# Dense products of a two-layer hybrid trunk: both correction passes in f16, with scaled weights and operands

## The chip, the cores and the metric

The kernel runs on one core of one Trainium2 chip. The metric is the device time of one execution in microseconds (us); less is better.

## What is computed

The reference takes x (1 x 512 x 1024, float32) through two layers. Cut to what matters:

```python
h = layer_norm(x, ln_in_g, ln_in_b)
for layer in range(2):
    proj = h @ w_in[layer]
    # split into the inputs of three mixers: retention, HGRN2, sliding-window attention
    y_a = (silu(rg) * r_o) @ ret_w_out[layer]
    y_b = (silu(hg) * h_o) @ hgrn_w_out[layer]
    y_c = s_o @ swa_w_out[layer]
    merged = sigmoid(ga) * y_a + sigmoid(gb) * y_b + sigmoid(gc) * y_c
    h = layer_norm(DN_ALPHA * h + merged @ w_o[layer], ln_mix_g[layer], ln_mix_b[layer])
    if layer == 0:
        ff = (silu(h @ w_gate) * (h @ w_up)) @ w_down          # dense, width 2816
    else:
        ff = top-2-of-8 experts of the same form               # width 3584
    h = layer_norm(DN_ALPHA * h + ff, ln_ffn_g[layer], ln_ffn_b[layer])
```

All weights arrive as float32 from DRAM.

## The kernel before, in words

Tokens are 512 = 4 blocks (j) of 128, D_MODEL is 8 slices (k) of 128. The residual stream is held transposed, as operand hT. To reach float32-like results, every dense operand is held in two parts: a high part, the value rounded to float32r (the type FR, which TensorE takes in one pass), and a low part, the remainder. A product is three matmuls into the same PSUM tile: high x high, high weight x low operand, low weight x high operand. mm3 (L347 to L350) issues these three; proj_t (L448) issues the same three itself at L457 to L459. I call three such matmuls a group. Before the change all three are float32r.

There are two forms of a product. proj_f (L418) holds a weight tile of 128 columns still and moves 512 tokens: 8 groups per tile. proj_t (L448) holds 128 tokens still and moves 512 weight columns: 32 groups (4 blocks x 8 slices) per product of depth 1024. proj_f_halves (L429) is used once, at the head of the FFN, with 256 tokens at a time; proj_t with 256 columns makes the values of the attention.

Weights come through the class Stream: SP loads a raw tile (L204, three buffers), and _prep (L211) makes its two parts: ScalarE writes whi with a Copy to float32r (L225), VectorE writes wlo as raw minus whi (L226). Five buffers of each part exist, and three tiles are prepared ahead. In the expert stage (the flag half) tiles are 2048 wide, scaled by WS, and wlo is f16 already (L221, L222); there the high parts run float32r and the low part of the weights runs f16, in blocks: accumulate (L1400) and by_row (L1459) issue all float32r matmuls of a tile first and then all f16 ones. by_row, used for the down projection of the last two experts, has eight float32r and four f16 matmuls of 512 columns per block.

Operands are split by split_evac (L343): ScalarE copies PSUM to the high part (L344), VectorE writes the low part (L345). It serves the transposed LayerNorm output (turn in ln_tile, L384), the branches of the three mixers (to_branch, L607, and the attention's values, L850). The merge (gate_merge, L900 and L901) and the FFN (L989 and L990) do the same from SBUF.

The order of TensorE's work is the order in which the code issues it: TensorE is in a manual schedule (L277). A helper (soon, tick) puts small attention and HGRN matmuls between products after a given amount of TensorE time. The order on ScalarE, VectorE and GpSimd is set by the scheduler of the tile framework. Each engine works its queue in order.

The program's stages: LayerNorm and the first product (to about 50 us), the attention of layer 0 (to about 200), HGRN heads (to about 400), gates, retention and merge (to 860), the dense FFN (to 1240), the same mixers for layer 1 (to 2080), and routing and experts (to the end). LayerNorm (ln_tile, L363) works on VectorE, ScalarE (L373) and GpSimd (L375, which adds ln_b); its blocks are transposed on TensorE (L388) when a product first needs them.

Of the kernel before, what the change touches and what calls it, by code (L numbers as in the profile page):

```python
# [21 lines left out]
P = 128  # L22
D = 1024
S = 512
# [33 lines left out]
XS = 1.0 / 64.0  # L58

# [127 lines left out]
class Stream:  # L187


    def __init__(self, nc, raw, parts, ahead, half):  # L190
        self.nc, self.raw, self.parts, self.ahead, self.half = nc, raw, parts, ahead, half
        self.todo, self.loaded, self.ready, self.held = [], [], [], 0

# [17 lines left out]
    def _prep(self):  # L211
# [7 lines left out]
        lo = pool.tile([P, width], F16 if self.half else FR, name="wlo", bufs=bufs)  # L219
        if self.half:  # L220
            nc.scalar.activation(hi[:, :n], raw, AF.Copy, scale=WS)  # L221
            nc.vector.scalar_tensor_tensor(lo[:, :n], raw, WS, hi[:, :n].bitcast(F32),  # L222
                                           op0=OP.mult, op1=OP.subtract)
# [26 lines left out]
def body(tc, A, out, dbg=None):  # L250
# [86 lines left out]
    V.memset(eps_ln, LN_EPS)  # L337
    eps_rms = const.tile([P, 1], F32, name="eps_rms")
    V.memset(eps_rms, RMS_EPS)
# [23 lines left out]
    def ln_tile(pool, j, r, gb, bb, hT, to_out, after=None, spread=False):  # L363
        mv = pool.tile([P, 4], F32, name="ln_mv", bufs=2)
        V.bn_aggr(mv[:, 0:2], stats[j])
        SC.activation(mv[:, 2:3], mv[:, 1:2], AF.Sqrt, bias=eps_ln)
# [17 lines left out]
        def turn():  # L384
            for kk in range(2):
                tp = psM.tile([P, 4, P], F32, name="mx")
                for k in range(4):
                    T.transpose(tp[:, k], r[:, (4 * kk + k) * P:(4 * kk + k + 1) * P], ident)  # L388
                split_evac(tp, hT[0][:, 4 * kk:4 * kk + 4, j * P:(j + 1) * P],
                           hT[1][:, 4 * kk:4 * kk + 4, j * P:(j + 1) * P])  # L390
# [17 lines left out]
    def new_hT():  # L408
        hi = hpool.tile([P, KD, S], FR, name="hThi")
        lo = hpool.tile([P, KD, S], FR, name="hTlo")  # L410
        return hi, lo
# [6 lines left out]
    def proj_f(hT, kn=KD):  # L418
        need(*range(NJ))
        whi, wlo = stream.next()  # L420
        ps = psA.tile([P, S], F32, name="acc")
        for k in range(kn):
            sl = slice(k * P, (k + 1) * P)
            mm3(ps, whi[:, sl], wlo[:, sl], hT[0][:, k], hT[1][:, k], k == 0, k == kn - 1)
# [4 lines left out]
    def proj_f_halves(hT, n):  # L429
# [6 lines left out]
        for th in range(2):  # L436
            tk = slice(256 * th, 256 * th + 256)
            for i, (ps, (whi, wlo)) in enumerate(zip(pss, ws)):
                if th == 0 and i >= n - 2:
                    need(i - n + 4)  # L440
                for k in range(KD):
                    sl = slice(k * P, (k + 1) * P)
                    mm3(ps[:, tk], whi[:, sl], wlo[:, sl], hT[0][:, k, tk], hT[1][:, k, tk], k == 0, k == KD - 1)
# [4 lines left out]
    def proj_t(xT, kn, per, n, done=None):  # L448
# [5 lines left out]
        def tile_(j, k, w, q):  # L454
# [3 lines left out]
            T.matmul(pss[j], xT[0][:, k, tj], w[1][:, sl], start=False, stop=False)  # L458
            T.matmul(pss[j], xT[1][:, k, tj], w[0][:, sl], start=False, stop=(k == kn - 1))  # L459
# [25 lines left out]
    def out_ln(pool, xT, kn, per, g_ap, b_ap, nxt, after=None):  # L485
# [3 lines left out]
        SC.dma_start(bb, rows(b_ap))  # L489
        old = hbuf[0]  # L490
# [8 lines left out]
        def done(j, ps):  # L499
            sl = slice(512 * half, 512 * half + 512)  # L500
            V.scalar_tensor_tensor(rs[j][:, sl], rs[j][:, sl], ALPHA, ps, op0=OP.mult, op1=OP.add)
# [24 lines left out]
    for j in range(NJ):  # L526
# [3 lines left out]
        if j == 0:  # L530
# [3 lines left out]
            SY.dma_start(bb, rows(A["ln_in_b"]))  # L534
        else:
# [38 lines left out]
    def route_consts():  # L574
# [6 lines left out]
        SC.activation(rt[:, :, 0], raw, AF.Copy)  # L581
        V.tensor_tensor(rt[:, :, 1], raw, rt[:, :, 0].bitcast(F32), OP.subtract)
# [10 lines left out]
        routing[:] = [rt, tri, tok, ones, iota, eidx]  # L593


    def gated_norm(pool, o_j, n, gate_j, width):
# [5 lines left out]
        SC.activation(ss[:, 1, :n], ss[:, 0, :n], AF.Sqrt, bias=eps_rms, scale=1.0 / width)  # L602
# [4 lines left out]
    def to_branch(gate, c0, br, k):  # L607
# [4 lines left out]
        split_evac(tf, br[0][:, k], br[1][:, k])  # L612
# [179 lines left out]
    def swa(pool, layer, hT, br):  # L792
# [14 lines left out]
        for j, ps in enumerate(proj_t(hT, KD, 4, 256)):  # L807
            SC.activation(v[:, j], ps, AF.Copy)
# [41 lines left out]
        def values(g, j, pts):  # L850
# [5 lines left out]
            split_evac(po[rp], br[0][rp, gp * GQ:(gp + 1) * GQ, j * P:(j + 1) * P],  # L856
# [812 lines left out]
```

## Time and profile before

| | us |
|---|---|
| median of 3 runs | 3213.3 |
| lowest and highest run | 3211.13, 3214.2 |
| the profiled execution, as timed | 3213.63 |
| its span, from first to last instruction | 3211.6 |
| TensorE busy in it | 3083.2 |
| VectorE busy | 2002.6 |
| ScalarE busy | 1665.6 |
| GpSimd busy | 744.9 |

The span is what the views of the trace divide up; 2.0 us of the profiled execution lie outside it. PE is TensorE's matmul side, PEld its weight loads, DVE is VectorE, ACT is ScalarE, POOL is GpSimd, SP issues the weight DMAs. Matmuls are pipelined: the time from one start to the next is shorter than the time one lasts, and it is the former that adds up.

### The profile page before, as it was taken

To read this page: it belongs to the slowest core of one execution; us is meant where nothing else is said; L and a number is where in the kernel's file an instruction comes from. 1 tells how busy PE (TensorE), PEld (TensorE's weight loads), DVE (VectorE), ACT (ScalarE), POOL (GpSimd) and SP (SyncE) were. 2 spreads that over 40 slices of the span, in tenths; PEclk is the share of its full clock that TensorE was granted. 3 is DMA by queue.
4 is the path that set the end of the run, shared out by engine and by line. 5 is a ranking of instruction groups with operands and counts; after the bars stand their busy time and mean duration, and the time that the engine had idled before them with its cause. 6 is when DMAs were issued, how large, how long until landed. Compare 5 with 4: busy or idle time off the path is not lost. (4 is left out here: it accounts for less than half of the span.)

```text
span 3211.6 us, 50454 instructions
## 1 busy us (share of the span) xinstructions
PE 3083.2 (96%) x20186; PEld 2666.9 (83%) x20186; DVE 2002.6 (62%) x2387; ACT 1665.6 (52%) x2475; POOL 744.9 (23%) x541
## 2 busy tenths in 40 slices
PE   7999899999999999999899999969999999999996
PEld 6778788888888888777788888869999999999794
DVE  5766733334533325766833334469888898989998
ACT  4655333323332214664433333248778787888785
POOL 1243501101100001234500111114223242242442
PEclk9999999999999999999999999979999999999998
DMA  5112132222422333111222222359999999999995
GB/s 175 53 56 83 56 105 89 82 92 92 147 99 99 117 115 110 63 59 53 79 92 92 88 83 93 117 196 350 332 326 347 331 343 350 361 341 379 384 374 203
DMA packets 108463, 562.60 MB, mean 175 GB/s; under 512 B 13115, under 2 KB 13163, under 8 KB 75965
## 3 DMA queue, kind: packets, MB, share of 16 engines
q1 hardware_dynamic: 96768, 522.23, 45.2%
q10 hardware_dynamic: 6732, 24.34, 2.0%
q0 software_dynamic: 4720, 12.72, 1.2%
q8 instruction: 161, 2.64, 0.3%
q14 instruction: 82, 0.66, 0.1%
HBM read 545.39 MB, written 13.85 MB: 174 GB/s over the span
## 5 line engine op out<-in xcount | busy, mean ns | idle before, releaser
L222 DVE SCALAR_TENSOR_TENSOR wlo<-raw,whi 128x2048 f16<-128x2048 f32 (+1 forms) x348 | 786.2, 2265 | 86.7 <-ACT whi L221 85.2
L225 ACT ACTIVATE whi<-raw 128x1024 fp32r<-128x1024 f32 x314 | 332.6, 1060 | 833.4 <-PE acc L294 712.4
L226 DVE TENSOR_TENSOR wlo<-raw,whi 128x1024 fp32r<-128x1024 f32 x314 | 435.6, 1388 | 510.3 <-ACT whi L225 486.3
L221 ACT ACTIVATE whi<-raw 128x2048 fp32r<-128x2048 f32 (+1 forms) x348 | 642.1, 1848 | 57.3 <-PE gu L294 50.7
L294 PE MATMUL acc<-hThi,whi 128*128 128x512 f32 (+1 forms) x1312 | 510.2, 389 | 2.3 <-ACT hThi L344 2.3
L294 PE MATMUL acc<-hTlo,whi 128*128 128x512 f32 (+1 forms) x1312 | 506.5, 386 | 1.4 <-DVE hTlo L345 1.4
L294 PE MATMUL acc<-hThi,wlo 128*128 128x512 f32 (+1 forms) x1312 | 506.2, 386 | 0.0
L294 PE MATMUL gu<-xg,whi 128*128 128x288 f32 (+6 forms) x3584 | 496.0, 291 | 6.0 <-DVE gt L1428 2.7
L294 PEld LDWEIGHTS gu<-xg,whi 128*128 128x128 f32 x3584 | 453.8, 190 | 7.9 <-ACT whi L221 3.2
L1432 POOL TENSOR_TENSOR gs<-gs,gt 128x288 f32<-128x288 f32 (+6 forms) x112 | 255.6, 2282 | 583.9 <-ACT gs L1431 583.6
L294 PEld LDWEIGHTS <-wlo 128*128 128x128 f16 x4928 | 285.2, 98 | 23.3 <-DVE wlo L222 6.0
L294 PEld LDWEIGHTS acc<-hThi,whi 128*128 128x128 f32 x1312 | 248.8, 190 | 55.2 <-issue 4.9
L294 PEld LDWEIGHTS acc<-hTlo,whi 128*128 128x128 f32 x1312 | 248.7, 190 | 49.3 <-DVE hTlo L345 1.7
L294 PEld LDWEIGHTS acc<-hThi,wlo 128*128 128x128 f32 x1312 | 248.4, 189 | 49.6
L294 PE MATMUL gu<-xh,wlo 128*128 128x144 f16 (+6 forms) x3584 | 244.6, 221 | 1.8 <-DVE wlo L222 1.4
L294 PE MATMUL acc<-whi,hThi 128*128 128x512 f32 (+1 forms) x576 | 224.9, 390 | 0.4 <-ACT hThi L344 0.3
L294 PE MATMUL acc<-whi,hTlo 128*128 128x512 f32 (+1 forms) x576 | 220.3, 383 | 3.9 <-DVE hTlo L345 3.9
L294 PE MATMUL acc<-wlo,hThi 128*128 128x512 f32 (+1 forms) x576 | 219.9, 382 | 2.0 <-DVE wlo L226 2.0
L294 PE MATMUL gu<-hd,whi 128*128 128x288 f32 (+4 forms) x1344 | 194.2, 295 | 0.0
L294 PEld LDWEIGHTS gu<-hd,whi 128*128 128x128 f32 x1344 | 174.9, 189 | 0.3
L294 PE MATMUL acc<-brhi,whi 128*128 128x512 f32 x384 | 150.0, 391 | 0.0
L294 PE MATMUL acc<-brhi,wlo 128*128 128x512 f32 x384 | 149.5, 389 | 0.0
(288 smaller groups left out, 4395.2 us busy)
## 6 DMA issues: line engine op xcount, KB each, us to landing
raw<-in_w_gu SPq DMA_DIRECT2D x224, 1024.0 KB, 7.2
raw<-in_w_l SPq DMA_DIRECT2D x248, 512.0 KB, 3.4
raw<-in_w_dn SPq DMA_DIRECT2D x96, 896.0 KB, 5.6
raw<-in_w_ffn SPq DMA_DIRECT2D x66, 512.0 KB, 3.5
raw<-in_w_dr SPq DMA_DIRECT2D x28, 1024.0 KB, 7.7
hspillm<-ln_r ACTq DMA_DIRECT2D x8, 512.0 KB, 2.6
ybuf<-ys ACTq DMA_DIRECT2D x5, 512.0 KB, 9.3
ln_r<-in_x SPq DMA_DIRECT2D x4, 512.0 KB, 10.9
```

The source lines that it names most:

```text
L221: nc.scalar.activation(hi[:, :n], raw, AF.Copy, scale=WS)
L222: nc.vector.scalar_tensor_tensor(lo[:, :n], raw, WS, hi[:, :n].bitcast(F32), op0=OP.mult, op1=OP.subtract)
L225: nc.scalar.activation(hi[:, :n], raw, AF.Copy)
L226: nc.vector.tensor_tensor(lo[:, :n], raw, hi[:, :n].bitcast(F32), OP.subtract)
L294: nc.tensor.matmul(out_, lhsT, rhs, start=start, stop=stop)
L1432: G.tensor_tensor(s, s, t[:, 1], OP.mult)
```

## The change

Dense weights are scaled by DS = 256 and operands by factors of LS = 16, so that remainders and copies fit f16. A weight tile now has three parts: whi (float32r), the remainder in f16 (the first half of the tile named wlo), and an f16 copy of the weight divided by LS (the second half of wlo). An operand has three parts as well: high (float32r), low (f16), and an f16 copy (named hT16, br16, hid16, fin16). mm3 and proj_t issue high x high in float32r, weight remainder x operand copy in f16, weight copy x operand remainder in f16. The producers of operands put the scales into constants that their instructions take: scales of LayerNorm and of the RMS norms, the factors of gates and FFN. The number of matmuls and their shapes stay the same. The expert stage changes in constants only.

```diff
@@ Stream._prep
         hi = pool.tile([P, width], FR, name="whi", bufs=bufs)
-        lo = pool.tile([P, width], F16 if self.half else FR, name="wlo", bufs=bufs)
+        lo = pool.tile([P, 2048], F16, name="wlo", bufs=bufs)
+        scale = WS if self.half else DS
+        nc.scalar.activation(hi[:, :n], raw, AF.Copy, scale=scale)
+        nc.vector.scalar_tensor_tensor(lo[:, :n], raw, scale, hi[:, :n].bitcast(F32), op0=OP.mult, op1=OP.subtract)
         if self.half:
...
+            self.ready.append((hi, lo))
         else:
-            nc.scalar.activation(hi[:, :n], raw, AF.Copy)
-            nc.vector.tensor_tensor(lo[:, :n], raw, hi[:, :n].bitcast(F32), OP.subtract)
-        self.ready.append((hi, lo))
+            if self.early:
+                nc.gpsimd.tensor_scalar(lo[:, 1024:1024 + n], raw, 1.0 / LS, None, op0=OP.mult)
+            else:
+                nc.scalar.activation(lo[:, 1024:1024 + n], raw, AF.Copy, scale=1.0 / LS)
+            self.ready.append((hi, lo, lo[:, 1024:]))
@@ body
-    def split_evac(ps, hi, lo, src_f32=None):
-        SC.activation(hi, ps, AF.Copy)
-        V.tensor_tensor(lo, ps, hi.bitcast(F32), OP.subtract)
-
-    def mm3(ps, whi, wlo, xhi, xlo, first, last):
-        T.matmul(ps, whi, xhi, start=first, stop=False)
-        T.matmul(ps, whi, xlo, start=False, stop=False)
-        T.matmul(ps, wlo, xhi, start=False, stop=last)
+    def split(src, hi, lo, x16):
+
+        SC.activation(hi, src, AF.Copy, scale=1.0 / (DS * LS))
+        SC.activation(x16, src, AF.Copy, scale=1.0 / (DS * LS))
+        V.scalar_tensor_tensor(lo, hi.bitcast(F32), -DS * LS, src, op0=OP.mult, op1=OP.add)
+
+    def mm3(ps, w, x, first, last):
+        T.matmul(ps, w[0], x[0], start=first, stop=False)
+        T.matmul(ps, w[1], x[2], start=False, stop=False)
+        T.matmul(ps, w[2], x[1], start=False, stop=last)
@@ proj_t
-            T.matmul(pss[j], xT[0][:, k, tj], w[1][:, sl], start=False, stop=False)
-            T.matmul(pss[j], xT[1][:, k, tj], w[0][:, sl], start=False, stop=(k == kn - 1))
+            T.matmul(pss[j], xT[2][:, k, tj], w[1][:, sl], start=False, stop=False)
+            T.matmul(pss[j], xT[1][:, k, tj], w[2][:, sl], start=False, stop=(k == kn - 1))
@@ out_ln, and the same line in the first norm
+        V.tensor_scalar(bb, bb, LS, None, op0=OP.mult)
@@ dense_ffn
-                V.tensor_tensor(t, pu, t, OP.mult)
-                SC.activation(hi[:, f], t, AF.Copy)
-                V.tensor_tensor(lo[:, f], t, hi[:, f].bitcast(F32), OP.subtract)
+                V.scalar_tensor_tensor(t, pu, LS, t, op0=OP.mult, op1=OP.mult)
+                split(t, hi[:, f], lo[:, f], x16[:, f])
```

The flag early is False and nothing sets it, so ScalarE makes the copy of every weight. In gate_merge and dense_ffn a tensor_tensor becomes a scalar_tensor_tensor with LS as its factor; the router gets an f16 copy of its weights.

The order of matmuls on TensorE is the same in both kernels, and so are SP's DMAs. What an f16 matmul adds is an instruction of its own that loads the held operand; there are 5184 of them. On TensorE, at the end of the first product (rows one to three of the first listing are the last group of proj_t, the rest the first of proj_f; mm3 has the same form), before:

```order
L294 MATMUL acc<-whi,hThi 128x512
L294 MATMUL acc<-wlo,hThi 128x512
L294 MATMUL acc<-whi,hTlo 128x512
L294 MATMUL acc<-hThi,whi 128x512
L294 MATMUL acc<-hTlo,whi 128x512
L294 MATMUL acc<-hThi,wlo 128x512
```

and in the changed kernel, where hT_89 is the f16 copy of hT:

```order
L302 MATMUL acc<-whi,hThi 128x512
L302 LDWEIGHTS hT_89
L302 MATMUL acc<-wlo,hT_89 128x512
L302 LDWEIGHTS hTlo
L302 MATMUL acc<-wlo,hTlo 128x512
L302 MATMUL acc<-hThi,whi 128x512
L302 LDWEIGHTS wlo
L302 MATMUL acc<-hT_89,wlo 128x512
L302 LDWEIGHTS wlo
L302 MATMUL acc<-hTlo,wlo 128x512
```

Every group is now one float32r matmul and two f16 ones, so the type changes twice in a group.

On VectorE, in the first LayerNorm (ln_r are the token blocks, ln_mv their statistics, hTlo the low parts of the transposed output), before:

```order
L365 BN_AGGR ln_mv<-ln_st 128x2
L345 TENSOR_TENSOR hTlo<-mx,hThi 128x4x128
L226 TENSOR_TENSOR wlo<-raw,whi 128x1024
L374 TENSOR_TENSOR ln_r<-ln_r,ln_g 128x512 x2
L367 RECIPROCAL ln_mv<-ln_mv 128x1
L369 SCALAR_TENSOR_TENSOR ln_mv<-ln_mv 128x1
L226 TENSOR_TENSOR wlo<-raw,whi 128x1024
L345 TENSOR_TENSOR hTlo<-mx,hThi 128x4x128
L374 TENSOR_TENSOR ln_r<-ln_r,ln_g 128x512 x2
L345 TENSOR_TENSOR hTlo<-mx,hThi 128x4x128 x5
```

and in the changed kernel:

```order
L357 SCALAR_TENSOR_TENSOR hTlo<-hThi,mx 128x4x128
L227 SCALAR_TENSOR_TENSOR wlo<-raw,whi 128x1024 x2
L387 TENSOR_TENSOR ln_r<-ln_r,ln_g 128x512 x2
L377 BN_AGGR ln_mv<-ln_st 128x2
L387 TENSOR_TENSOR ln_r<-ln_r,ln_g 128x512 x2
L380 RECIPROCAL ln_mv<-ln_mv 128x1
L382 SCALAR_TENSOR_TENSOR ln_mv<-ln_mv 128x1
L227 SCALAR_TENSOR_TENSOR wlo<-raw,whi 128x1024
L387 TENSOR_TENSOR ln_r<-ln_r,ln_g 128x512 x2
L357 SCALAR_TENSOR_TENSOR hTlo<-hThi,mx 128x4x128 x7
```

One low part is written before the norms of the four blocks are done, and seven after the last of them; before, three of the eight stood ahead of the last block's norm. The scaling of ln_b stands earlier in the same queue, ahead of the first block's scalar_tensor_tensor on ln_mv.

On ScalarE, in the FFN (fg is the gate, hidhi the hidden operand), before:

```order
L989 ACTIVATE hidhi<-fg 128x512
L225 ACTIVATE whi<-raw 128x1024
L986 ACTIVATE fg<-acc 128x512
L225 ACTIVATE whi<-raw 128x1024
L989 ACTIVATE hidhi<-fg 128x512
```

and in the changed kernel:

```order
L1003 ACTIVATE fg<-acc 128x512
L234 ACTIVATE wlo<-raw 128x1024
L226 ACTIVATE whi<-raw 128x1024
L234 ACTIVATE wlo<-raw 128x1024
L355 ACTIVATE hidhi<-fg 128x512
L356 ACTIVATE hid_6799<-fg 128x512
L226 ACTIVATE whi<-raw 128x1024
```

Each weight tile and each operand tile has one more copy in the queue.

## Rows read from the trace of the kernel before

**Rows 1.** The page's busy list: busy us, share of the span, instructions.
```profile
PE 3083.2 (96%) x20186; PEld 2666.9 (83%) x20186; DVE 2002.6 (62%) x2387; ACT 1665.6 (52%) x2475; POOL 744.9 (23%) x541
```

**Rows 2.** Busy time by stretch: us, each engine's busy us (instructions), granted clock, DMA.
```profile
85.00:200.00 115.00, 110.15 (x538) 81.74 (x537) 81.19 (x167) 81.26 (x214) 32.57 (x21) 1.00 0.16 51
200.00:400.00 200.00, 187.93 (x990) 156.41 (x989) 132.21 (x202) 84.92 (x181) 89.46 (x109) 0.97 0.20 68
400.00:860.00 460.00, 460.00 (x2086) 380.48 (x2085) 178.54 (x207) 152.24 (x223) 49.44 (x40) 1.00 0.29 98
890.00:1235.00 345.00, 345.00 (x1554) 286.78 (x1553) 121.54 (x137) 97.27 (x118) 8.79 (x6) 1.00 0.31 107
...
1610.00:2070.00 460.00, 460.00 (x2095) 381.05 (x2094) 170.63 (x192) 151.22 (x230) 43.68 (x37) 1.00 0.28 95
```

**Rows 3.** Groups of instructions by shape: xcount, busy us, mean ns of one, idle before.
```profile
L294 PE MATMUL acc<-hThi,whi 128*128 128x512 f32 x1248 | 490.8, 393 | 0.0
...
L294 PE MATMUL acc<-whi,hThi 128*128 128x512 f32 x512 | 206.8, 404 | 0.4 <-ACT hThi L344 0.3
...
L294 PE MATMUL acc<-brhi,whi 128*128 128x512 f32 x384 | 150.0, 391 | 0.0
...
L294 PE MATMUL acc<-whi,hidhi 128*128 128x512 f32 x176 | 68.6, 389 | 0.0
...
L294 PE MATMUL acc<-whi,finhi 128*128 128x512 f32 x128 | 51.7, 404 | 0.0
```

**Rows 4.** TensorE in order of time, FFN down projection: start us, us, instruction.
```profile
1149.79 0.39 PE L294 MATMUL acc<-whi,hidhi 128*128 128x512 f32 x1
...
1152.51 0.39 PE L294 MATMUL acc<-whi,hidhi 128*128 128x512 f32 x1
```

**Rows 5.** TensorE in order of time, down projection of the last expert.
```profile
3179.73 0.38 PE L294 MATMUL gu<-wlo,hh 128*112 128x512 f16 x1
3179.76 2.19 PE L294 MATMUL gu<-whi,hd 128*112 128x512 f32 x8
3181.79 1.02 PE L294 MATMUL gu<-wlo,hh 128*112 128x512 f16 x4
3182.47 2.20 PE L294 MATMUL gu<-whi,hd 128*112 128x512 f32 x8
```

**Rows 6.** TensorE in order of time, end of the first mixer's output product.
```profile
859.76 0.39 PE L294 MATMUL acc<-whi,finhi 128*128 128x512 f32 x1
...
862.56 0.39 PE L294 MATMUL acc<-whi,finhi 128*128 128x512 f32 x1
```

**Rows 7.** One tile's instructions: xcount, ns min/median/max, first and last start us, forms.
```profile
L222 DVE SCALAR_TENSOR_TENSOR wlo<-raw,whi x348: 2007/2281/2870, 2099.7 to 3180.6; 128x2048 f16<-128x2048 f32 x126, 128x1792 f16<-128x1792 f32 x48
L225 ACT ACTIVATE whi<-raw x314: 1040/1061/1083, 13.4 to 2059.8; 128x1024 fp32r<-128x1024 f32 x157
...
L344 ACT ACTIVATE brhi<-mx x64: 579/592/622, 109.6 to 1963.6; 64x512 fp32r<-64x512 f32 x32, 128x512 fp32r<-128x512 f32 x32
```

**Rows 8.** Waits of TensorE up to 2100 us: us in total, times, longest us.
```profile
PE mx L294 <- ACT adiag L733: 15.1, 5, 5.9
```

**Rows 9.** All engines in order of time, first LayerNorm and first product.
```profile
24.39 0.63 DVE L345 TENSOR_TENSOR hTlo<-mx,hThi 128x512 fp32r<-128x512 f32 x1
...
25.08 0.50 PE L294 MATMUL acc<-whi,hTlo 128*128 128x512 f32 x1 [1.22 <-DVE hTlo L345]
...
32.93 1.22 DVE L374 TENSOR_TENSOR ln_r<-ln_r,ln_g 128x512 f32<-128x512 f32 x1 [0.70 <-ACT ln_r L373]
...
49.87 0.39 PE L294 MATMUL acc<-hThi,whi 128*128 128x512 f32 x1
```

**Rows 10.** TensorE in order of time, an expert in the middle (264 and 132 columns).
```profile
2752.52 2.19 PE L294 MATMUL gu<-xg,whi 128*128 128x264 f32 x16
...
2761.31 1.94 PE L294 MATMUL gu<-hd,whi 128*128 128x264 f32 x14
...
2769.04 0.60 PE L299 MATMUL mx<-ident,xt 126*128 126x126 f32 x4
```

More of the change, by code (lines that the diff above doesn't have):

```diff
@@ L365, in ln_tile @@
         V.bn_aggr(mv[:, 0:2], stats[j])
-        SC.activation(mv[:, 2:3], mv[:, 1:2], AF.Sqrt, bias=eps_ln)
+        up = 1.0 if to_out is not None else LS
+        SC.activation(mv[:, 2:3], mv[:, 1:2], AF.Sqrt, bias=eps_out if to_out is not None else eps_ln, scale=1.0 / up ** 2)
         V.reciprocal(mv[:, 2:3], mv[:, 2:3])
@@ L388, in turn @@
                     T.transpose(tp[:, k], r[:, (4 * kk + k) * P:(4 * kk + k + 1) * P], ident)
-                split_evac(tp, hT[0][:, 4 * kk:4 * kk + 4, j * P:(j + 1) * P],
-                           hT[1][:, 4 * kk:4 * kk + 4, j * P:(j + 1) * P])
+                split(tp, *[t[:, 4 * kk:4 * kk + 4, j * P:(j + 1) * P] for t in hT])
             if after is not None:
@@ L409, in new_hT @@
         hi = hpool.tile([P, KD, S], FR, name="hThi")
-        lo = hpool.tile([P, KD, S], FR, name="hTlo")
-        return hi, lo
+        lo = hpool.tile([P, KD, S], F16, name="hTlo")
+        x16 = hpool.tile([P, KD, S], F16, name="hT16")
+        return hi, lo, x16
     def new_hbuf(n):
@@ L419, in proj_f @@
         need(*range(NJ))
-        whi, wlo = stream.next()
+        w = stream.next()
         ps = psA.tile([P, S], F32, name="acc")
@@ L423, in proj_f @@
             sl = slice(k * P, (k + 1) * P)
-            mm3(ps, whi[:, sl], wlo[:, sl], hT[0][:, k], hT[1][:, k], k == 0, k == kn - 1)
+            mm3(ps, [t[:, sl] for t in w], [t[:, k] for t in hT], k == 0, k == kn - 1)
         tick()
@@ L437, in proj_f_halves @@
             tk = slice(256 * th, 256 * th + 256)
-            for i, (ps, (whi, wlo)) in enumerate(zip(pss, ws)):
+            for i, (ps, w) in enumerate(zip(pss, ws)):
                 if th == 0 and i >= n - 2:
@@ L611, in to_branch @@
         tf = tp.rearrange("p a b -> p (a b)")
-        split_evac(tf, br[0][:, k], br[1][:, k])
+        split(tf, *[t[:, k] for t in br])
     def token_major(tok, name, hT, func, pss=None):
@@ L855, in values @@
                 T.matmul(po[rp], v[:, j - 1 + u, 64 * g:64 * g + 64], pt, start=(u == pts[0][0]), stop=(u == 1))
-            split_evac(po[rp], br[0][rp, gp * GQ:(gp + 1) * GQ, j * P:(j + 1) * P],
-                       br[1][rp, gp * GQ:(gp + 1) * GQ, j * P:(j + 1) * P])
+            split(po[rp], *[t[rp, gp * GQ:(gp + 1) * GQ, j * P:(j + 1) * P] for t in br])
         values.prio = 1
@@ L899, in gate_merge @@
                     G.tensor_tensor(sg, mg[d], sg, OP.add)
-                    SC.activation(fin[0][:, d], sg, AF.Copy)
-                    V.tensor_tensor(fin[1][:, d], sg, fin[0][:, d].bitcast(F32), OP.subtract)
+                    split(sg, *[t[:, d] for t in fin])
             if d + GATE_AHEAD < KD:
@@ L906, in pair @@
         hi = pool.tile([P, KD, S], FR, name=name + "hi", bufs=1)
-        lo = pool.tile([P, KD, S], FR, name=name + "lo", bufs=1)
-        return hi, lo
+        lo = pool.tile([P, KD, S], F16, name=name + "lo", bufs=1)
+        x16 = pool.tile([P, KD, S], F16, name=name + "16", bufs=1)
+        return hi, lo, x16
     def mixers(layer, hT, g_ap, b_ap, after=None):
@@ L980, in dense_ffn @@
         hi = pool.tile([P, KF, S], FR, name="hidhi")
-        lo = pool.tile([P, KF, S], FR, name="hidlo")
+        lo = pool.tile([P, KF, S], F16, name="hidlo")
+        x16 = pool.tile([P, KF, S], F16, name="hid16")
         with tc.tile_pool(name="act", bufs=1, reuse_waits="tile") as lp:
```

47 lines of the change are left out of this document (26 added, 21 removed).

## The prediction, made before the changed kernel was timed

> **What bounds the kernel now.** I read the page's busy list first: TensorE is busy 96% of the span [rows 1]. The table of stretches then tells where that binds [rows 2]. From 400 to 860, from 890 to 1235 and from 1610 to 2070 us TensorE is busy for the whole stretch, with ScalarE at 152, 97 and 151 us: there the end is set by how far apart matmuls start, and nothing else. In the sliding-window attention (85 to 200) it is busy 110 of 115 us with ScalarE at 81, in the HGRN heads (200 to 400) 188 of 200: there some waits end last. After 2150 us come the experts, whose matmuls the change does not touch. So the question is what one group of three matmuls costs before and after, and what the added ScalarE work does where TensorE is not alone.
>
> The groups are counted in the list of groups [rows 3]: 1248 + 512 + 384 + 176 + 128 = 2448 groups of three at 512 columns (each row is one of a group's three). Another 128, at 256 columns, are left out of the sum: at 0.01 us each they are 1 us.
>
> **A group now.** In the FFN's down projection twelve matmuls, four groups, start in 1152.51 - 1149.79 = 2.72 us: 0.680 us a group, 0.227 us a matmul [rows 4].
>
> **A group after.** One float32r matmul stays, two become f16 at the same 512 columns. The kernel before has such f16 matmuls in its last two experts, in blocks of eight float32r and four f16 [rows 5]. One f16 matmul alone lasts 0.38 us and four in a row 1.02 us, so they start (1.02 - 0.38)/3 = 0.213 us apart; with two-digit rows 0.213 to 0.217, I take 0.215. The change of type has its price in the same rows: a block of twelve takes 3182.47 - 3179.76 = 2.71 us. With float32r matmuls at 0.227 us, 8 x 0.227 + 4 x 0.215 = 2.68 would leave 0.03 us for the two changes of type; but with heavy DMA traffic float32r matmuls alone are slower, as at the end of the first mixer: twelve in 862.56 - 859.76 = 2.80 us, 0.233 each [rows 6]. With 0.233 nothing is left. The experts' tail has heavy traffic too, so I take a value near the lower end, c = 0.005 us for the two changes, and keep 0 and 0.03 as ends. A group is then 0.227 + 2 x 0.215 + 0.005 = 0.662 us: 0.018 us less (between 0.023 less and 0.007 more).
>
> All 2448 groups: 44 us (56 less to 17 more). By the code 32 + 80 + 224 groups of each layer lie in the first product, the attention and the HGRN stage, 672 in all; the other 1776 lie where TensorE is never idle and keep their gain, 32 us. Of the 12 us of the 672 I count half, since waits end last in part of them. **Gain: 38 us.** The 5184 more weight-load instructions that the order shows are inside the measured f16 spacing, since the experts' f16 matmuls are issued the same way.
>
> **ScalarE.** Each of 314 weight tiles gets a third copy. Its nearest row is the existing copy of the same tile, 1.061 us [rows 7]: 333 us. Each split gets a second copy of 0.592 us [rows 7]: 64 for branches, 32 for hT, 22 for the FFN, 16 for the merge, 134 x 0.592 = 79 us. In the three saturated stretches this adds well under the idle time of ScalarE, which is over 60% there [rows 2], and tiles are prepared three ahead of some 5.4 us each (8 groups x 0.68): no cost. If that cover went, it would be TensorE waiting for a weight tile. In the attention a layer has 12 weight tiles and 16 outputs: 12 x 1.06 + 16 x 0.59 = 22 us on top of 81 in 115 us, 90% busy. The softmax chain is queued behind these copies on the same engine. Bounds: nothing (34 us are idle now), and all 22 us a layer. Nearer to nothing, as the two transposing steps of a unit are ordered 12 us of TensorE time behind its scores: 3 us a layer, **6 us**. In the HGRN stage TensorE waits 15.1 us for ScalarE's diagonal copies over both layers [rows 8], themselves behind VectorE; a weight copy of 1.06 us can be in front in each of 16 heads, 0 to 17 us: **2 us**. At three layer ends two second copies stand in the chain from LayerNorm to the next product, 3 x 2 x 0.59: **4 us**.
>
> **VectorE.** The weight remainders change form; half of the experts' 2048-wide form, 2.281 / 2 = 1.14 us [rows 7], is no longer than what it replaces, and VectorE is 39% busy or less in the saturated stretches: nothing. The other products keep their lengths; the added scalings by constants ride in instructions that exist, except that of ln_b, one per norm.
>
> **The start.** Here the new order costs. The fifth group needs the second half of block 0's low part; before it came at 24.39 and the group's last matmul went at 25.08, with 27 of 32 groups to go until 49.87 [rows 9]. In the new order the remaining seven low parts stand on VectorE behind the norms of all four blocks, of which the last was done at 32.93 + 1.22 = 34 us [rows 9]; ScalarE's third copies and ln_b's scaling push the norms back, the low parts that no longer stand between them pull them forward. I take 33.5 for the fifth group's last matmul. What is left, 27 groups and three transposing steps of 1 us, takes 27 x 0.662 + 3 = 21 us, to 54.5: 5 us late, and I add 1 us for the pause itself, **6 us** (2 to 10).
>
> **Sum.** -38 + 6 + 2 + 4 + 6 = -20 us. The profiled execution took 3213.6 us, 0.3 above the median of the runs; 3213.6 - 20 = 3193.6, I say **3193 us**.
>
> **Rivals.**
> 1. *Each change of type costs (slower).* At small shapes it does. Blocks of 16 + 16 matmuls of 264 and 132 columns take (2761.31 - 2752.52)/3 = 2.93 us, blocks of 14 + 14 take (2769.04 - 2761.31)/3 = 2.58 [rows 10]: 0.353 us for two pairs, 2.83 for sixteen, so 0.10 us a block goes into the two changes. With c = 0.10 a group is 0.757 us: 2448 x 0.077 = 188, plus 18 of side costs, 3420 us; with c = 0.03, 17 + 18, 3249 us. It decides from c = 0.0145, where 2112 effective groups x (0.023 - c) is no more than 18. Against it: the 512-column block, where a change lies beside a matmul of over 0.2 us, leaves 0.03 at most. Chance 0.04.
> 2. *ScalarE becomes the bound outside the saturated stretches (slower).* If its present idle 34 us in the attention stay and 22 us come on top, that is 44 us in two layers; 17 in the HGRN heads, 10 at the start, 4 at the layer ends; less the 32 that are safe: +43, 3257 us. For it: 90% busy and one queue in order. Against: TensorE waits under 5 us there now. Chance 0.05.
> 3. *An f16 pass is no shorter than a float32r one in these products (the change does not do what it says):* the distance is set by 512 columns in either type, only side costs stay, 3213.6 + 18 = 3232 us. Rows 4 and 5 differ by 0.012 us a matmul, in stages with different neighbours. Chance 0.03. The Trainium skill (TensorE: Matmul & The Clock Gate, Weight-path perf modes) says that the array processes one element per cell per cycle whatever its width, and by that rule the 44 us would be nothing. The rows here speak against it for float32r, by those 0.012 us.
> 4. *Consecutive f16 matmuls overlap further.* A spacing of 0.131 us would save 2448 x 2 x 0.096 = 470 us: 2762 us with the side costs. Chance 0.01. The same page (Back-to-back issue gap) gives such a figure for 512 columns in a stream of loads and matmuls; the rows of the experts' tail show 0.215 us for just such a stream.
>
> **How the numbers follow.** The forecast has 0.87. Within it the gain runs from some 50 down to nothing with c and the side costs: 0.76 is faster by over 0.2% (6.4 us, about what a measurement of this kernel can tell), 0.08 within it, 0.03 slower. Rivals 1 to 3 add 0.12 to slower, rival 4 0.01 to faster: 0.77, 0.08, 0.15. The range reaches from c = 0 with small side costs, 46 us less, 3167 us, to the taken c with side costs of 42 us, halfway from 18 towards their worst sum (10 + 44 + 17 + 8), 3218 us; beyond lie some 0.05 below and 0.13 above.
>
> **What would show it.** Right: groups of the FFN 0.66 us apart (8 of them 5.3 instead of 5.4), f16 matmuls 0.215 us after one another, the saturated stretches some 2.5% shorter, the first product's end near 55 instead of 49.9 us, attention stretches no shorter. Wrong: groups at 0.68 or more; TensorE waits on weight copies; waits in attention and HGRN of over 20 us more. The experts' stretch must keep its length.

## The result, and the profile after

The changed kernel takes 3231.9 us, median of 6 runs (3230.3 to 3233.3); the kernel before, on the same chip, 3213.2. The ratio is 1.0059, 95% interval 1.0048 to 1.0070: 19 us slower. The forecast was 3193 us, with 3167 to 3218 as the range.

The busy list of the page, to set beside [rows 1]: 

```profile
PE 3074.4 (95%) x20186; PEld 2028.8 (63%) x20186; DVE 1968.9 (61%) x2393; ACT 2013.1 (62%) x2921; POOL 774.7 (24%) x541
```

The same number of matmuls, TensorE as busy as before, and 348 us more work on ScalarE. The table of stretches (us, busy us of PE, PEld, DVE, ACT, POOL with instructions, granted clock, DMA share, GB/s), against [rows 2]; the last line is the place in this kernel of the matmuls that [rows 2] has from 400 to 860:

```profile
85.00:200.00 115.00, 108.91 (x543) 58.85 (x541) 78.33 (x163) 89.45 (x224) 29.63 (x18) 1.00 0.17 55
200.00:400.00 200.00, 182.87 (x933) 100.17 (x931) 133.08 (x196) 114.50 (x213) 89.18 (x106) 0.96 0.22 69
400.00:860.00 460.00, 460.00 (x2120) 226.22 (x2119) 158.64 (x200) 233.77 (x330) 62.30 (x43) 1.00 0.29 97
...
416.90:874.40 457.50, 457.50 (x2085) 222.60 (x2084) 161.79 (x207) 233.79 (x322) 63.47 (x40) 1.00 0.30 98
```

Where TensorE had been the only bound it still is: 460 of 460 us, although ScalarE went from 152 to 234. The kernel is 17 us late by then, so the same window of the clock shows other work. The same matmuls take 457.5 us where they took 460, 0.5% less; the forecast spacing would have been 2.7% shorter.

TensorE in order of time in the FFN's down projection, five groups of three, against [rows 4] (start us, us, instruction):

```profile
1165.08 0.58 PE L302 MATMUL acc<-whi,hidhi 128*128 128x512 f32 x1
1165.50 0.39 PE L302 MATMUL acc<-wlo,hid 128*128 128x512 f16 x1
1165.73 0.38 PE L302 MATMUL acc<-wlo,hidlo 128*128 128x512 f16 x1
1165.76 0.58 PE L302 MATMUL acc<-whi,hidhi 128*128 128x512 f32 x1
...
1168.47 0.58 PE L302 MATMUL acc<-whi,hidhi 128*128 128x512 f32 x1
```

Five groups take 1168.47 - 1165.08 = 3.39 us, 0.678 each. That is 0.002 less than the 0.680 of [rows 4], where 0.018 less was forecast. From the first f16 matmul to the second it is 0.23 us, not 0.215; how the other 0.45 us divide at the float32r matmul can't be read, since its recorded start lies 0.03 us behind that of the matmul before it.

Where the 19 us arise is seen by comparing matmuls of the same number, as both kernels issue the same 20186 (us behind the kernel before, worked out from the two traces; columns by the time in the kernel before):

| kernel | 50 (first product ends) | 220 | 238 (first HGRN head) | 400 | 860 | 890 (layer end) | 1235 | 1610 | 2070 | 3189 |
|---|---|---|---|---|---|---|---|---|---|---|
| changed | 10.9 | 12.2 | 17.6 | 16.9 | 14.4 | 16.8 | 15.9 | 18.4 | 15.9 | 16.9 |
| no weight copies | 3.3 | 5.2 | 11.8 | 9.9 | 7.4 | 9.3 | 8.4 | 10.6 | 8.1 | 10.0 |
| no operand copies | 8.1 | 8.5 | 8.3 | 8.1 | 5.6 | 8.1 | 7.2 | 6.8 | 4.3 | 3.0 |
| neither | 2.1 | 0.8 | 0.6 | 1.2 | -1.3 | -1.6 | -2.5 | -7.2 | -9.7 | -10.8 |
| attention's copies on GpSimd | 12.2 | 12.6 | 12.4 | 12.2 | 9.7 | 12.2 | 11.3 | 10.5 | 8.0 | 9.7 |

The other kernels are those of the experiments below. In the changed kernel the loss comes in steps, at the start, at the first HGRN head and at layer ends; the saturated stretches give back only 2.5 us (400 to 860), 0.9 and 2.5. The start, all engines in order of time (in brackets the idle time before, and what ended it):

```profile
17.28 1.11 PE L307 MATMUL mx<-ident,ln_r 128*128 128x128 f32 x4 [1.09 <-POOL ln_r L388]
...
24.68 2.92 ACT L386 ACTIVATE ln_r<-ln_r,ln_mv 128x512 f32<-128x512 f32 x4
...
29.73 3.21 ACTq L395 DMA_DIRECT2D hspillin<-ln_r  x2
33.05 0.30 ACT L379 ACTIVATE ln_mv<-ln_mv,eps_ln 128x1 f32<-128x1 f32 x1 [5.45 <-POOL ln_r L388]
...
34.19 1.50 ACT L386 ACTIVATE ln_r<-ln_r,ln_mv 128x512 f32<-128x512 f32 x2
...
35.60 1.04 ACT L234 ACTIVATE wlo<-raw 128x1024 f16<-128x1024 f32 x1
36.55 0.57 ACT L355 ACTIVATE hThi<-mx 128x512 fp32r<-128x512 f32 x1
...
37.18 0.79 PE L302 MATMUL acc<-whi,hThi 128*128 128x512 f32 x1 [10.59 <-ACT hThi L355]
```

and in the kernel before, the same copy of the high part:

```profile
17.05 0.59 ACT L344 ACTIVATE hThi<-mx 128x512 fp32r<-128x512 f32 x1
```

TensorE waits 10.59 us for the second half of the first block's high part, whose transposes were done at 18.39. That copy (36.55) stands on ScalarE behind norm instructions of the other blocks (24.68 to 35.60), behind stores that wait for GpSimd, and behind four of the new weight copies (the last at 35.60). In the forecast this pause was put down to VectorE's low parts [rows 9]; they were not last. The pause is followed by a slow stretch of TensorE:

```profile
37.10:41.00 3.90, 3.82 (x12) 2.07 (x13) 0.69 (x1) 0.50 (x2) 2.00 (x2) 0.52 0.69 246
41.00:50.00 9.00, 9.00 (x48) 4.79 (x47) 2.58 (x4) 5.11 (x10) 0.00 (x0) 1.00 0.03 10
```

After 11 us nearly without a matmul the granted clock is 0.52, close to the lower of its two levels (1.2 GHz), and the group that starts at 38.43 takes until 40.09, 1.66 us; from 41 us on the clock is 1.00 and a group takes 0.68. So about 1 us of the start's loss lies in that one group.

### The profile page after: what moved, and what is told of

Its sections match the earlier page's. It is cut to its first block, busy times and chain, and to the rows that moved or that the text cites. A ratio compares the mean times of both kernels' runs of the same rounds, so it can differ in the third digit from the quotient of the medians.

```text
span 3228.5 us, 51045 instructions
## 1 busy us (share of the span) xinstructions
PE 3074.4 (95%) x20186; PEld 2028.8 (63%) x20186; DVE 1968.9 (61%) x2393; ACT 2013.1 (62%) x2921; POOL 774.7 (24%) x541
## 3 DMA queue, kind: packets, MB, share of 16 engines
q8 instruction: 161, 2.64, 0.3%
## 5 line engine op out<-in xcount | busy, mean ns | idle before, releaser
L227 DVE SCALAR_TENSOR_TENSOR wlo<-raw,whi 128x1024 f16<-128x1024 f32 (+2 forms) x662 | 1178.0, 1783 | 561.9 <-ACT whi L226 559.8
L226 ACT ACTIVATE whi<-raw 128x1024 fp32r<-128x1024 f32 (+2 forms) x662 | 973.5, 1472 | 601.2 <-PE acc L302 471.8
L302 PEld LDWEIGHTS <-wlo 128*128 128x128 f16 x8320 | 481.5, 98 | 441.0 <-issue 413.2
L302 PE MATMUL acc<-hThi,whi 128*128 128x512 f32 (+1 forms) x1312 | 747.9, 570 | 4.6 <-ACT hThi L355 4.6
L302 PE MATMUL acc<-hT,wlo 128*128 128x512 f16 (+1 forms) x1312 | 507.6, 387 | 0.1
L302 PE MATMUL acc<-hTlo,wlo 128*128 128x512 f16 (+1 forms) x1312 | 493.0, 376 | 1.9 <-DVE hTlo L357 1.9
L234 ACT ACTIVATE wlo<-raw 128x1024 f16<-128x1024 f32 x314 | 329.2, 1049 | 6.4 <-POOL ln_r L388 3.2
L302 PE MATMUL acc<-wlo,hT 128*128 128x512 f16 (+1 forms) x576 | 220.9, 384 | 2.2 <-DVE wlo L227 2.1
L302 PE MATMUL acc<-wlo,hTlo 128*128 128x512 f16 (+1 forms) x576 | 214.5, 372 | 0.3 <-DVE hTlo L357 0.3
L302 PE MATMUL acc<-br,wlo 128*128 128x512 f16 x384 | 149.8, 390 | 0.0
## 6 DMA issues: line engine op xcount, KB each, us to landing
ln_r<-in_x SPq DMA_DIRECT2D x4, 512.0 KB, 10.5
```

Of the source, the lines that this page charges most:

```text
L226: nc.scalar.activation(hi[:, :n], raw, AF.Copy, scale=scale)
L227: nc.vector.scalar_tensor_tensor(lo[:, :n], raw, scale, hi[:, :n].bitcast(F32), op0=OP.mult, op1=OP.subtract)
L234: nc.scalar.activation(lo[:, 1024:1024 + n], raw, AF.Copy, scale=1.0 / LS)
L302: nc.tensor.matmul(out_, lhsT, rhs, start=start, stop=stop)
```

## Experiments

Ratios are to the kernel before, run on the same chip beside each; differences between kernels are those of the ratios or of medians.

### Order of the matmuls: blocks of eight groups, and of two

In proj_f (proj_t likewise); mm_r issues the first matmul of mm3, mm_h the other two:

```diff
-        for k in range(kn):
-            sl = slice(k * P, (k + 1) * P)
-            mm3(ps, [t[:, sl] for t in w], [t[:, k] for t in hT], k == 0, k == kn - 1)
+        for k0 in range(0, kn, 8):
+            ks = range(k0, min(k0 + 8, kn))
+            for k in ks:
+                sl = slice(k * P, (k + 1) * P)
+                mm_r(ps, [t[:, sl] for t in w], [t[:, k] for t in hT], k == 0)
+            for k in ks:
+                sl = slice(k * P, (k + 1) * P)
+                mm_h(ps, [t[:, sl] for t in w], [t[:, k] for t in hT], k == kn - 1)
```

Blocks of eight:

> The changed kernel with its dense matmuls in blocks: the eight float32r matmuls of a weight tile first, then its sixteen f16 ones (in proj_t all tiles of a step likewise). Same matmuls, same copies. Theory Change (in the changed kernel each group of three takes 0.677 us because the step from float32r to f16 and back costs 0.019 us a group, which eats the gain): one pair of changes in eight groups is left, a group falls to 0.227 + 0.430 + 0.019/8 = 0.659 us, 2112 to 2448 groups by 0.017 us give back 36 to 41 us, about 3193 us; inside the f16 block matmuls start 0.215 us apart. Rival Width (an f16 matmul of 512 columns with a held operand of 128 columns takes as long as a float32r one, whatever stands beside it): 3232 us, f16 matmuls 0.226 us apart in the block too. Rival Copies (the groups are shorter, but ScalarE's copies hold TensorE up for as much): 3230 us or more, with TensorE idle before blocks.

Measured 3215.0 us, ratio 1.0008 (0.9999 to 1.0017): 17 us of the change's 19 come back, less than half of what theory Change gave. Blocks of two, the same with 2 in place of 8:

> The changed kernel with two float32r matmuls and then four f16 ones: blocks of two groups instead of eight. Theory Change: half the changes are left, a group takes 0.227 + 0.430 + 0.0095 = 0.667 us, 18 to 21 us less than the changed kernel, about 3213 us, halfway between it and the blocks of eight. Rival Width: 3232. Rival Copies: 3230 or more.

Measured 3227.2 us, 1.0053 (1.0039 to 1.0066): 5 us come back, where theory Change had 18 to 21. TensorE in the blocks of eight, FFN down projection:

```profile
1155.32 0.39 PE L302 MATMUL acc<-wlo,hid 128*128 128x512 f16 x1
1155.55 0.38 PE L302 MATMUL acc<-wlo,hidlo 128*128 128x512 f16 x1
1155.77 0.38 PE L302 MATMUL acc<-wlo,hid 128*128 128x512 f16 x1
...
1158.57 0.38 PE L302 MATMUL acc<-wlo,hidlo 128*128 128x512 f16 x1
1158.60 2.19 PE L302 MATMUL acc<-whi,hidhi 128*128 128x512 f32 x8
1160.63 0.39 PE L302 MATMUL acc<-wlo,hid 128*128 128x512 f16 x1
```

and in the blocks of two:

```profile
1160.60 0.39 PE L302 MATMUL acc<-wlo,hid 128*128 128x512 f16 x1
...
1163.29 0.39 PE L302 MATMUL acc<-wlo,hid 128*128 128x512 f16 x1
```

A group takes (1160.63 - 1155.32)/8 = 0.664 us in blocks of eight, (1163.29 - 1160.60)/4 = 0.673 in blocks of two, 0.678 alone. So part of a group is paid once per block: 0.678 - 0.664 = 7/8 of 0.016, and blocks of two save less than half of it. From the second on, f16 matmuls start (1158.57 - 1155.55)/14 = 0.216 us apart; only the first takes 0.23. Rival Width falls in its simple form.

2448 groups by 0.014 are 34 us, and 17 arrived. Half of the rest was lost before 400 us: there this kernel is 3.7 us behind the changed one (by matmuls of the same number), where 336 groups should have put it 4.7 ahead. The other half went to new waits behind that; that they come from eight float32r matmuls in front, which ask for eight high parts at once, is argued and not shown. TensorE's waits between 800 and 1300 us in blocks (us, times, longest):

```profile
PE acc L302 <- ACT whi L226: 6.9, 2, 4.4
PE acc L302 <- ACT hThi L355: 5.0, 1, 5.0
PE acc L302 <- ACT finhi L355: 2.1, 1, 2.1
```

In the changed kernel the first is 0.8 us, the second 4.6, and the third is not there: some 9 us more of waiting.

### The width of the held operand

[Rows 5], from which the price of the change of type was taken, read "128*112": there the f16 matmuls hold 112 columns. The dense ones hold 128. Two kernels narrow the f16 matmuls, of each group the first alone, or both; they leave the products of the other 16 columns out of the correction:

```diff
-        T.matmul(ps, w[1], x[2], start=False, stop=False)
+        T.matmul(ps[:112], w[1][:, :112], x[2], start=False, stop=False)
```

> The changed kernel with the first f16 matmul of each group, the one right behind the float32r matmul, holding 112 of its 128 columns (the products of the other 16 columns are left out of that correction). The price of the change of type was read from the last experts, whose f16 matmuls hold 112 columns, and the dense ones hold 128. If the price belongs to a held f16 operand of 128 columns behind a float32r matmul: f16 to f16 0.215 instead of 0.227 us, a group about 0.665 to 0.669 us, 20 to 30 us less than the changed kernel, 3202 to 3212 us. If the change of type costs the same at any width: 3228 to 3234 us, a group 0.677 to 0.680.

> As the one before, but both f16 matmuls of a group hold 112 columns (the last group of a product excepted for its second f16 matmul). If a held f16 operand of 128 columns behind float32r is the cause: a group 0.660 to 0.665 us, 3195 to 3205 us, and no shorter than the one before by more than 0.005 us a group, since only the first f16 matmul follows a float32r one. If width plays no part: 3228 to 3234 us.

Measured 3196.2 us, 0.9951 (0.9935 to 0.9968), for the first alone, and 3193.5 us, 0.9943 (0.9926 to 0.9959), for both: no clear difference between the two. Changed kernel to first alone: 36 us less, more than expected if the width is the cause. So the width matters in the matmul right behind the float32r one, and in the other it does not. Same place of the program, in the kernel with the first alone:

```profile
1157.44 0.58 PE L302 MATMUL acc<-whi,hidhi 128*128 128x512 f32 x1
1157.86 0.38 PE L302 MATMUL acc<-wlo,hid 128*112 128x512 f16 x1
1158.08 0.38 PE L302 MATMUL acc<-wlo,hidlo 128*128 128x512 f16 x1
...
1160.08 0.58 PE L302 MATMUL acc<-whi,hidhi 128*128 128x512 f32 x1
```

Four groups in 1160.08 - 1157.44 = 2.64 us, 0.660 each, with both changes of type still in every group. Why, the weight loads tell. In the changed kernel:

```profile
1165.50 0.10 PEld L302 LDWEIGHTS <-hid 128*128 128x128 f16 x1 [0.26 <-issue]
1165.51 0.10 PEld L302 LDWEIGHTS <-hidlo 128*128 128x128 f16 x1
1165.73 0.19 PEld L302 LDWEIGHTS acc<-whi,hidhi 128*128 128x128 f32 x1
1166.17 0.10 PEld L302 LDWEIGHTS <-hid 128*128 128x128 f16 x1 [0.25 <-issue]
```

and with 112 columns:

```profile
1158.08 0.19 PEld L302 LDWEIGHTS acc<-whi,hidhi 128*128 128x128 f32 x1
1158.29 0.13 PEld L302 LDWEIGHTS <-hid 128*112 128x112 f16 x1
1158.52 0.10 PEld L302 LDWEIGHTS <-hidlo 128*128 128x128 f16 x1
1158.74 0.19 PEld L302 LDWEIGHTS acc<-whi,hidhi 128*128 128x128 f32 x1
```

With 112 columns the load goes 0.21 us after the float32r load ahead of it, under the running float32r matmul. With 128 it sits idle 0.25 us and starts 0.44 us after that load (1165.73 to 1166.17), together with its own matmul at 1166.18: that load is not hidden. Between two f16 matmuls it is (1165.51). The list of groups showed it in one line of the changed kernel's page:

```profile
L302 PEld LDWEIGHTS <-wlo 128*128 128x128 f16 x8320 | 481.5, 98 | 441.0 <-issue 413.2
```

Here "issue" is idle time for which the profile shows no releaser, 413 us; in the kernel with 112 columns the group of that name has 1.7. This is idle time of the loads, not time lost: a group of matmuls loses 0.018 us by it. The Trainium skill (TensorE: Matmul & The Clock Gate, Weight-path perf modes) says that the fast weight load is on when 128 weights are loaded and the type is not FP32. The durations agree, 0.10 us for 128 columns of f16 against 0.13 for 112 and 0.19 for float32. That a load of 128 columns does not start under a float32r matmul is what the rows show. Why the chip does so no run tells.

### The side work

The kernel before with the new side work alone, that is ScalarE's copies of weights and operands issued twice and ln_b multiplied by one:

```diff
-            nc.scalar.activation(hi[:, :n], raw, AF.Copy)
+            for _ in range(2):
+                nc.scalar.activation(hi[:, :n], raw, AF.Copy)
```

> The kernel before, with float32r corrections as they were, but with each of ScalarE's copies of weight tiles and of split operands issued twice (the same values again), and with ln_b multiplied by one at each norm: the side work of the change alone, at the old order of matmuls. Theory Change: the groups gain only 0.0035 us x 2448 = 8 us in the changed kernel, so side work costs what is left of +19: about 24 us here (18 to 30), 3237 us. Rival Copies: the groups gain 38 to 44 us and side work eats 57 to 63, so 3270 to 3276 us here. Rival Width: the groups gain nothing and side work costs 19, 3232 us.

Measured 3252.3 us, 1.0126 (1.0110 to 1.0141): 39 us, between the theories. It is not the change's side work exactly: the second copy is written to the high part, so its readers wait for it too. The cleaner way is to take copies out of the changed kernel, the weights', the operands', and both:

```diff
...
-                nc.scalar.activation(lo[:, 1024:1024 + n], raw, AF.Copy, scale=1.0 / LS)
-            self.ready.append((hi, lo, lo[:, 1024:]))
+            self.ready.append((hi, lo, lo))
```
```diff
-        SC.activation(x16, src, AF.Copy, scale=1.0 / (DS * LS))
...
-        return hi, lo, x16
+        return hi, lo, lo
```

> The changed kernel without the f16 copies of the weights: the third matmul of a group takes the f16 low part of the weights once more, so this product is left out of the result; the number and shapes of matmuls are the same. It bounds what the weight copies cost on any engine. Theory Weight copies: 3232 less 15 to 22, 3210 to 3217 us, with start, attention and HGRN heads near their lengths before. Theory Operand copies: 3226 to 3232 us.

> The changed kernel without the second copies of split operands (norm outputs, branches, FFN hidden rows, merged rows): the second matmul of a group takes the f16 low part of the operand instead of the f16 copy, so this product of the result is wrong by what it leaves out; matmuls are the same in number and shape, the weights' copies stay. Leaving out the weights' copies gave 8 us, nearly all at the start. Theory Operand copies (they stand between a norm, a head or a branch and the next product): 8 to 15 us less than the changed kernel, 3217 to 3224 us, with the layer ends and the HGRN heads back near their lengths before. Theory Order (the instructions of VectorE come in another order since the operations differ, and the delays follow from that): 3228 to 3233 us.

> The changed kernel in its own order, groups of three, without the f16 copies of weights and of operands (both f16 matmuls of a group take the f16 low parts, so these two products are left out of the result). Beside the bare blocks' 3184.6 us it prices the order of the matmuls alone, without any of the new ScalarE work. Theory Change: the blocks are worth 0.0166 us a group less what their own order costs in waits, 25 to 38 us, so 3209 to 3222 us here; adding up what the two kinds of copies cost when left out one at a time (8 and 14.5) gives 3209. If the copies were what hid the f16 gain (theory Copies): 3185 to 3195 us, as short as in blocks.

Measured: without weight copies 3224.0 us, 1.0032 (1.0019 to 1.0044); without operand copies 3217.4, 1.0017 (1.0008 to 1.0026); without both 3201.6, 0.9966 (0.9952 to 0.9979). The first and the third lie between their theories, the second is where theory Operand copies put it. The weights' 314 copies cost 8 us, nearly all at the start (10.9 against 3.3 in the first two rows of the table); the operands' 134, a quarter of the time, cost 14: the step at the first HGRN head, 3 us at the start, the rest in the second layer and after it. Both together cost 30, more than 8 + 14; that each fills idle time that the other leaves would fit, but no run shows it. Without any side work the change is 11.6 us faster than the kernel before; by the table 5.9 of them come in the three saturated stretches, and where the others come from no run shows. The same without copies, in blocks of eight:

> Blocks of eight and sixteen, without the f16 copies of weights and of operands (both f16 matmuls of a group take the f16 low parts, so these two products are left out of the result): the new matmuls without the new ScalarE work. If the blocks' gain per group of 0.0166 us holds for all 2448 groups it is 41 us, and with copies gone only the new order on VectorE and the scaling of ln_b stay: 3213 - 41 + 5 to 15 = 3177 to 3187 us. If the copies cost little even in blocks: 3205 us or more.

Measured 3184.6 us, 0.9920 (0.9906 to 0.9933): 17 us less than in groups of three by the medians, 15 by the ratios: within the noise as much as with the copies.

### Moving the copies

The first ln_b on GpSimd, by G.tensor_scalar for V.tensor_scalar:

> The changed kernel with the first norm's ln_b scaled on GpSimd instead of VectorE; all else as in the changed kernel. In the changed kernel VectorE waits at 8.65 us for ln_b to land before it can go on with the first norm, and the first transposes start at 15.1 instead of 9.8 us. Theory Change takes the start for 11 of the 19 us, and this wait for about 5 of the 11: 3224 to 3229 us, first transposes near 10 us. If the 11 us come from the third copies and the new order alone: 3232 us, even where the first transposes come earlier.

Measured 3230.5 us, 1.0056 (1.0043 to 1.0070). GpSimd takes 2.78 us for it; transposes start at 12.7 us instead of 15.1, and 1.4 us are left of it, which the measurement can't tell from nothing. The weights' copies on VectorE, by nc.vector.tensor_scalar, and on GpSimd, by early = True:

> The changed kernel with each weight tile's f16 copy made on VectorE instead of ScalarE; all else as changed. The blocks of eight showed that the groups gain 0.017 us each once the changes of type are gone, but gave 17 us where the saturated stretches alone gave 25, so side work costs more than my 18. Theory Weight copies (the 314 third copies on ScalarE are what delays the start, the attention and the HGRN heads): most of some 25 us of side work goes, less some for VectorE's own load: 3212 to 3220 us. Theory Operand copies (the second copies of split operands, which stand in the chains from a norm or a head to the next product, and the new order on VectorE): 3228 to 3234 us.

> The changed kernel with each weight tile's f16 copy made on GpSimd. GpSimd's 512-wide addition takes 1.9 us, so a 1024-wide copy may take 2 to 4 us, under the 5.4 us of a tile in the saturated stretches, but GpSimd has the norm's additions at the start and products in the attention. Theory Weight copies: HGRN heads and attention get back some 10 us, the start loses some 5: 3222 to 3232 us. Theory Operand copies: 3232 to 3245 us.

Measured 3238.5 us, 1.0082 (1.0068 to 1.0095), and 3272.8, 1.0184 (1.0168 to 1.0199): both slower than on ScalarE. VectorE's copy takes 0.84 us, GpSimd's 2.83, and both theories missed the two results, the first by 4 us at least and the second by 28. By matmuls of the same number GpSimd's copies lose 23 us between 220 and 400 us and 19 between 1235 and 1610, the HGRN stages and the attention before the second. Then the attention's 32 operand copies on GpSimd, which takes 0.61 us for one:

```diff
+            G.tensor_copy(x16, hi.bitcast(F32))
```

> The changed kernel with the second copy of the attention's outputs (32 of 128 by 512 in both layers) made on GpSimd from the high part, instead of on ScalarE; the others stay. Leaving out all operand copies took away 6 us of waiting in the first HGRN head and gave 14.5 us in all. If ScalarE's queue in the attention is the cause: 6 to 8 us less than the changed kernel, 3224 to 3226 us, with no step of delay at the first HGRN head. If it is the other operand copies or VectorE's order: 3229 to 3233 us. GpSimd is itself in the chain of that head, so a loss of some us is possible too.

Measured 3225.4 us, 1.0040 (1.0027 to 1.0054): 6.5 us less. TensorE's waits at the first HGRN head, in the changed kernel (236 to 262 us):

```profile
PE mx L302 <- DVE ql L732: 4.0, 1, 4.0
```

and here (225 to 260 us):

```profile
PE mx L302 <- ACT adiag L753: 0.7, 1, 0.7
```

So ScalarE's operand copies in the attention made the head's inputs on VectorE late. The order of copy and low part was tried too, by exchanging the last two lines of split:

> The changed kernel with the two last lines of split exchanged: high part, then VectorE's low part, then ScalarE's f16 copy. Same instructions. In the changed kernel's trace VectorE's low parts of branches waited 54.3 us for the second copy, in 51 cases, though they need only the first. If operand copies cost time because the low part stands behind them: 6 to 12 us less, 3220 to 3226 us. If they cost ScalarE's time wherever they stand: 3229 to 3234 us.

Measured 3239.1 us, 1.0079 (1.0065 to 1.0093), 7 slower, which neither theory had: the second matmul of a group now waits for the f16 copy, 15.8 us at the start, where the changed kernel waited 10.6 for the high part. The step at the first HGRN head stays, though (18.3 us behind at 220 us, 24.0 at 238), so at the head the low part's place behind the copy is not what costs; what stays the same in this kernel is the copies' time on ScalarE.

### A version that beats both

Blocks of eight, but groups of three where an operand's last part comes late; weights' copies on VectorE until the first product has ended, on ScalarE from there; the first ln_b on GpSimd (first run); the attention's own products in groups of three as well (second); and the attention's operand copies on GpSimd (third):

```diff
+            ps = proj_f(br, grouped=(d == 0))
...
+        pss = proj_t(hT, KD, 2, 512)
+        stream.early = False
```

> Blocks of eight and sixteen, but groups of three in the two places where an operand's last part comes late (the first column of a product's last stage, the first product on a branch); f16 copies of the weights on VectorE until the first product has ended and on ScalarE from there; the first ln_b scaled on GpSimd. From the blocks' 3215: 7 us for the start, as VectorE's copies gave there, and 3 for the waits on late parts: 3203 to 3208 us. If the delays only move on, 3212 to 3216 us.

> As the one before, and the attention's own products in groups of three as well: the blocks of eight lost 3 to 4 us in the attention against the changed kernel. 3200 to 3206 us if the block order is the cause; 3203 to 3209 us, no better than the one before, if it is the order on VectorE.

> The best version so far (blocks of eight, groups of three in the attention and where parts come late, weights' copies on VectorE at the start) with the attention's operand copies on GpSimd too. If ScalarE's queue in the attention is what delays the first HGRN head: 3190 to 3193 us; else 3196 to 3200 us.

Measured 3200.8 us, 0.9968 (0.9955 to 0.9980); 3197.2, 0.9960 (0.9946 to 0.9973); 3190.1, 0.9932 (0.9919 to 0.9946). The last is 23 us faster than the kernel before and computes all three products of every group. An earlier one, with VectorE's copies throughout and blocks everywhere, took 3215.4 us (expected 3198 to 3204), and had the first ln_b on GpSimd too.

## Why the prediction was wrong

- **A group now, 0.680 us, and where it binds**: right. The saturated stretches stayed TensorE's alone, and ScalarE's copies cost nothing in them: the kernel with neither kind of copy gains the same 2.5, 0.9 and 2.5 us there.
- **An f16 matmul at 0.215 us**: right, 0.216 in blocks. The Trainium skill's figure for a stream of loads and matmuls (TensorE: Matmul & The Clock Gate, Back-to-back issue gap), about 0.131 us a matmul at 512 columns, is rival 4; no order here came near it.
- **c = 0.005 us for the two changes of type: the step that failed.** Its rows, [rows 5], hold 112 columns and the term is for 128. In the forecast's terms c is 0.678 - (0.227 + 2 x 0.215) = 0.021 us, of which 0.678 - 0.660 = 0.018 is the width; with 112 columns 0.003 is left. That is above the 0.0145 from which rival 1 decides, and inside the 0.03 kept as the end. With 0.021 the forecast's own sum is 2112 x (0.023 - 0.021) = 4 us of gain, where 38 were expected; the three saturated stretches gave 5.9. The blocks of [rows 10], which hold 128 columns, spoke of 0.10, five times what came; I set them aside for their size and did not look at the width.
- **Heavy DMA traffic as the reason to take c near nothing: wrong.** While the matmuls of [rows 5] ran, the DMA moved nothing. The last two numbers of a line are DMA share and GB/s, here for [rows 4], [rows 6] and [rows 5] in the kernel before:

```profile
1149.70:1152.60 2.90, 2.90 (x15) 2.39 (x14) 0.16 (x1) 1.06 (x1) 0.00 (x0) 1.00 0.41 151
859.00:863.00 4.00, 4.00 (x18) 3.21 (x18) 3.08 (x8) 3.79 (x6) 1.44 (x1) 1.00 0.32 131
3179.70:3182.50 2.80, 2.80 (x15) 1.97 (x13) 2.80 (x2) 0.00 (x0) 0.00 (x0) 1.00 0.00 0
```

  What puts float32r matmuls 0.233 us apart in [rows 6] is open; in [rows 4], with more traffic, they are 0.227 apart. For 112 columns the value taken was near the 0.003 measured, and that was luck.
- **Side costs of 18 us: too low.** The copies alone cost 30. The start was said to cost 6, with the fifth group's last matmul at 33.5 us and the end near 55; they were 38.4 and 60.7. The mechanism was wrong as well: I followed VectorE's low parts, and ScalarE's high part came last. HGRN was given 2 us for copies in front of the diagonal ones [rows 8]; those waits stayed as they were, and 5.4 us came at the first head by copies issued in the attention before it. The attention itself, 6 forecast, lost some 4 (1.4 and 2.4 us by the same comparison); the first two layer ends lost 2.4 us each and the third 1, where 1.2 each were forecast.
- **The sum**: with c = 0.021 and the 18 us of side costs the forecast would have been 14 us slower, 3228 us, beyond its range and 4 us from the result. So of the 39 us between forecast and result 34 are c, and some 5 the side work. The runs divide it as 30 for the copies less 11.6 for the rest, which makes the measured 19 by construction; in this division the 5.7 us that no run explains stand against the copies. The upper end of the range has a slip too: halfway from 18 to 79 is 48.5 and not 42, which gives 3224 us, and the result lies beyond that as well.
- **Rivals**: rival 1 came true in kind, at a price between the 0.0145 from which it decides and the 0.03 of its smaller case; I gave it 0.04. Rival 3's 3232 us is the measured time, but not for its reason: f16 matmuls are shorter. Rival 2 did not come: ScalarE is 62% busy, 78% in the attention (85 to 200 us), and it costs by single late copies, not as a bound.

## What to carry to other kernels

A row that prices an operation must match in what the price hangs on: the width of the held operand stood in the row and was read over. Where matmuls of two types alternate, look at the weight loads' idle time with releaser "issue", and put matmuls of one type together, except where an operand's last part arrives late. An engine that is 60% busy still costs: ask for each added copy which one-off chain (start, stage's first head, layer end) it stands in.

## What was not expected of the hardware

An f16 weight load of 128 columns (0.10 us) does not start while a float32r matmul of 512 columns runs, one of 112 columns (0.13 us) does; so the narrower operand, with the longer load, makes the group 0.018 us shorter. And in blocks of eight, float32r matmuls take (5.31 - 15 x 0.216 - 0.23)/8 = 0.23 us each, no shorter than in [rows 4].
